# Nine of 32 experts multiply unsplit float32 weights; ranks mixed piece by piece; results collected by column halves

## The chip, the cores and the metric

One core of a Trainium2 chip runs the whole program in one launch. The metric is the device time of an execution in microseconds (us). PE is the matrix engine, PEld its weight loads, DVE, ACT and POOL are the vector, scalar and GpSimd engines, SP issues most of the DMAs.

## The reference

Two transformer blocks follow each other. The first ends in a mixture of experts, and that is what the change touches:

```
logits = h @ w_router + b_router            # 512 tokens, 32 experts
top 4 experts of each token, gates = softmax of their logits
f[token] = sum over its 4 experts e of gate * ((swiglu(h @ w1[e] + b1[e])) @ w2[e] + b2[e])
# w1[e]: [1024, 2048], w2[e]: [1024, 1024], all float32
x = layer_norm(alpha * x + gt2 * f)
```

`swiglu` clamps pairs of columns, multiplies a sigmoid with them and leaves 1024 columns. All 32 experts' weights are read: 32 x 12 MB.

## The kernel before

**Ranks and rows.** The experts are sorted by how many tokens chose them. `CAP` (line 1246) gives the rank its rows: 192 for ranks 0 to 5, 128 for ranks 6 to 14, 64 for ranks 15 to 31. A rank of 192 is worked as a block of 128 and a block of 64.

**Tiles and pieces.** `Weights` (line 1282) streams weights as tiles `wraw` of two chunks of 128 rows by 512 columns (512 KB). Seven such buffers exist. `split` (line 1299) makes two float32r parts of each tile: ACT rounds it into `whi` (L1308), DVE (736 of the 1024 columns, L1312) and POOL (288, L1313) subtract into `wlo`. Up to three tiles are split ahead of their use. Four tiles are a piece: an expert has four pieces of the first product (0 to 3) and two of the second (4, 5), 24 tiles in all, so the stage has 768 tiles.

**Products.** `mm_part` (line 1669) makes, for each of a tile's two chunks, products of 128x512 in float32r: rows' high part by `whi` (L1675), by `wlo` (L1676), and, for a block of 128 rows, rows' low part by `whi` (L1678). For a block of 64 rows both parts lie side by side in one stationary operand, and two products do. So a tile takes 4 products for a rank of 64, 6 for 128, 10 for 192. A piece of the first product begins with a small product that adds the bias (L1803). `swiglu` (line 1680) follows, and its result is transposed and split (L1666, L1667); `down` (line 1811) scales the second product by the gate and splits it into `y`.

**Order.** `sequence` (line 1254) puts ranks into groups and `order` (line 1269) writes down by hand the order of a group's pieces; A, B, C are the ranks of the group. Before: six groups of [192, 64, 64] rows, and between them two of [128, 128] and five of [128, 64]:

```
[192, 64, 64]   A0 B0 B1 A1 B2 B3 A2 C0 C1 A3 B4 C2 C3 A4 B5 A5 C4 C5
[128, 64]       A0 A1 B0 A2 B1 A3 B2 B3 A4 A5 B4 B5
```

A rank's token rows are fetched by an indirect DMA from POOL into `xg` (L1649, three buffers) and transposed on PE (L1662); a table `at`, made in `experts` (line 1755), says before which piece. After a group's last piece, `collect` (line 1864) adds its results to the tokens' accumulators: products with one-hots (L1879) and additions on DVE (L1888).

Of the kernel before, what the change touches and what calls it, by code (L numbers as in the profile page):

```python
# [22 lines left out]
def consts1():  # L23
# [6 lines left out]
    dft = np.concatenate([np.cos(ph)[:, :257] * s, np.sin(ph)[:, 1:256] * s], 1).astype(np.float32)      # [512, 512]  # L30
    dfc = np.concatenate([np.cos(pc), np.sin(pc)], 1).astype(np.float32)          # [64, 128]
# [6 lines left out]
    m = np.concatenate([strict, incl, -strict], 1)                                        # [64 s, (a | r | -a) t]  # L38
    m = np.concatenate([m, m], 0)                                                # both halves of the rows
# [11 lines left out]
def rsqrt(nc, x, y, h, t):  # L51
    """x [p, m] -> 1/sqrt(x) in place, by three steps of Newton's."""
# [33 lines left out]
def ahead(loads, parts):  # L86
    """Each load one part ahead of its use."""
# [11 lines left out]
class Blk1:  # L99
# [13 lines left out]
    # ---- parameters  # L113
    def params(self, tmp):
# [26 lines left out]
        # derived columns  # L141
        self.mq = c.tile([128, 32], F, name="muq")          # mu / 4, 1 - mu
# [15 lines left out]
    # ---- modulation  # L158
# [100 lines left out]
    def memory(self, pool):  # L259
        """Pieces: the second block's memory, its rows normed and transposed -> memD."""  # L260
# [37 lines left out]
    def stats(self, x, pool):  # L298
        """mean and 1/std columns of the rows of x [128, 1024]"""
# [7 lines left out]
    def front(self):  # L307
        tc, nc, I, c = self.tc, self.nc, self.i, self.c
        self.x0 = self.dram.tile([512, 1024], F, name="x0D")
        with tc.tile_pool(name="fh", bufs=1) as hp, tc.tile_pool(name="ft", bufs=1) as tmp, tc.tile_pool(name="fw", bufs=2) as wp:  # L310
# [4 lines left out]
            with tc.tile_pool(name="fx", bufs=1) as xp, tc.tile_pool(name="fwa", bufs=4) as wr:  # L315
# [10 lines left out]
                # alpha (gains, biases) on all partitions  # L326
# [48 lines left out]
            def shift(pl, pcx, ch, dst_l, dst_c):  # L375
                """Token shift of the channels ch of the projections (psums), to the destinations."""
# [26 lines left out]
            def group(c0, n, ctx, evac):  # L403
                """Parts for the channels c0 .. c0+n; evac(j, psum lat, psum ctx)"""
# [54 lines left out]
            def spill(dst, j, t):  # L459
                """Channels t [128, ctx | lat] -> parts of 128 tokens in the order of either direction."""  # L460
# [53 lines left out]
    def norm_keys(self, pool, spill):  # L514
        """kn = k k_k / max(|k k_k|, 1e-12) per head"""
# [31 lines left out]
    def get(self, u, k):  # L547
        return self.U[u][k] if u < 6 else []
# [31 lines left out]
    def ttile(self, shape, name):  # L580
        """Tiles of 4 KB, in turn; some of their places come with the second pool."""
# [12 lines left out]
    def unit(self, u):  # L594
        """The parts of two chunks of either direction (n = direction, chunk) that don't need the state."""
# [10 lines left out]
        def lora(i):  # L606
            def f():
                w, src, nm = ((self.w2[0], self.lw, "sw"), (self.w2[1], self.la, "a"))[i]
                dst = S[nm] = self.tt(nm)
                for d in range(2):  # L610
# [9 lines left out]
                    for hp in range(4):  # L620
                        # sigmoid(x) = (1 + tanh(x / 2)) / 2; the halves of the biases are in hb
# [88 lines left out]
        def solve(a, b):  # L710
            # even rows on the first half of the partitions, odd rows on the second
# [67 lines left out]
    def chain(self, S):  # L779
        """The steps over the chunks, in pieces."""  # L780
# [120 lines left out]
    def fourier(self):  # L901
        """Pieces of the Fourier mixing."""
# [26 lines left out]
        def third(ch, s):  # L929
            # cosines for the first half of the places (they are even), sines (odd)  # L930
# [19 lines left out]
    def rsqrt(self, x, n, eps, pool):  # L950
        """x [128, m] sums over n -> 1/sqrt(mean + eps), in place."""
# [6 lines left out]
    def gn_consts(self, p, rk):  # L958
        """Gains and bonus weights by rows, the gates' weights, in p [128, 2048] and rk [128, 2, 4, 8]."""
# [82 lines left out]
    def gn_pieces(self):  # L1042
        """Pieces of the group norm for all units but the last."""
# [71 lines left out]
    def output(self, rw, gn, W, pool, h2, hT, setup, each):  # L1115
        """x1 = LN(alpha x0 + gt1 mixed) -> DRAM, h2 = x1 (1 + sc2) + sh2 -> h2 and transposed hT; each(t) follows.
        rw: room for the parts of the recurrent half of the mixed channels; gn: what is left of it and the Fourier half."""
# [27 lines left out]
        def mm(p, t, kk, w, first, last):  # L1145
            """Two chunks from kk on."""
# [16 lines left out]
        # (W gives the weights in this order) the Fourier half of either columns, the recurrent half  # L1163
# [80 lines left out]
# rows that a rank gets without a branch: 128 + 64, 128, 64  # L1244
# [8 lines left out]

def sequence():
    """Ranks in groups worked on together, so that products and loads keep step; the first rank is known before the routing."""
    h, m, l = ([r for r in range(32) if CAP[r] == c] for c in (192, 128, 64))
    three = [[r, l.pop(0), l.pop(0)] for r in h]
    two = [[r, l.pop(0)] if l else [r] for r in m]
    one = [g[0] for g in two if len(g) == 1]
    two = [one[i:i + 2] for i in range(0, len(one), 2)] + [g for g in two if len(g) == 2]  # L1260
# [7 lines left out]
def order(g):  # L1268
    """Pieces of a group's products: 0 for the first, 1 for the second, rank, columns."""
    if len(g) == 1:  # L1270
        text = "A0 A1 A2 A3 A4 A5"
    elif len(g) == 2:
        text = "A0 A1 B0 A2 B1 A3 B2 B3 A4 A5 B4 B5"
    elif g[0] == 0:
        text = "A0 A1 B0 B1 B2 A2 B3 C0 A3 C1 B4 C2 C3 A4 B5 A5 C4 C5"
    else:
        text = "A0 B0 B1 A1 B2 B3 A2 C0 C1 A3 B4 C2 C3 A4 B5 A5 C4 C5"
# [1805 lines left out]
```

## Time and profile before

| | |
|---|---|
| runs | 3830.72, 3824.44, 3829.01 us, median 3829.01 us |
| profiled execution, span from first to last instruction | 3830.3 us |
| its own time against the median | the span is 1.3 us above the median and 0.4 us below the slowest run |
| busy over the span | PE 3391.2 (89%), DVE 2819.2 (74%), POOL 2035.1 (53%), ACT 1888.8 (49%) |
| experts' stage, first to last expert product | 822.1 to 2422 us |

The page cuts the span into 40 slices of 96 us; the experts' stage is slices 9 to 25. A line of the view by stretches holds the stretch and its length, then for PE, PEld, DVE, ACT and POOL the busy time and the number of instructions, then PE's granted clock as a share of 2.4 GHz, the busy share of the DMA engines and GB/s. A line by group holds line, engine, operation, out<-in, shapes, the count, the busy time, the mean ns of one, and the idle time ahead of them with what ended it. PE's instructions overlap, so what one costs in a row of them is the distance between starts.

### The profile page before, as it was taken

How to read it: one execution, taken by the hardware profiler on the slowest of the kernel's cores; microseconds unless marked ns; L12 is line 12 of the kernel's file. 1: busy time of each engine (PE TensorE's matmuls, PEld its weight loads, DVE VectorE, ACT ScalarE, POOL GpSimd, SP SyncE). 2: the span in 40 equal slices, each digit the busy share in tenths (PEclk: the TensorE clock that was granted, in tenths of full speed). 3: DMA queues.
4: the chain of work that ended last, by engine and by line, in shares of the span. 5: the costliest groups of instructions: out<-in, count | busy, mean ns of one | idle time of the engine just before them, and what ended most of it. 6: DMA issues, size and time to landing. Idle time of an engine off the chain costs nothing. (4 is left out here: it accounts for less than half of the span.)

```text
span 3830.3 us, 53524 instructions
## 1 busy us (share of the span) xinstructions
PE 3391.2 (89%) x17300; PEld 2590.0 (68%) x17300; DVE 2819.2 (74%) x5095; ACT 1888.8 (49%) x3153; POOL 2035.1 (53%) x1734
## 2 busy tenths in 40 slices
PE   7967689858998998888989887699999999999999
PEld 4756567645666766665666664488878878877887
DVE  6778865668998989998998988855566445555653
ACT  4634323235666666666666665443444434443442
POOL 4444323447678877887877887623242332334223
PEclk9976767868999999999999998899999999999999
DMA  7853243636788878888888887522231134223112
GB/s 253 263 138 82 65 102 91 210 118 224 250 266 262 289 258 274 274 266 262 269 283 258 261 270 259 178 82 81 72 86 50 56 122 121 78 67 90 44 50 105
DMA packets 420662, 654.00 MB, mean 171 GB/s; under 512 B 83939, under 2 KB 145568, under 8 KB 419862
## 3 DMA queue, kind: packets, MB, share of 16 engines
q1 hardware_dynamic: 414650, 633.32, 52.6%
q0 software_dynamic: 4000, 13.90, 1.2%
q8 instruction: 139, 2.28, 0.2%
q10 hardware_dynamic: 1724, 3.28, 0.2%
q14 instruction: 149, 1.22, 0.1%
HBM read 610.80 MB, written 39.61 MB: 170 GB/s over the span
## 5 line engine op out<-in xcount | busy, mean ns | idle before, releaser
L1313 POOL TENSOR_TENSOR wlo<-wraw,whi 128x288 fp32r<-128x288 f32 x952 | 1181.1, 1256 | 843.4 <-ACT whi L1308 777.6
L1312 DVE TENSOR_TENSOR wlo<-wraw,whi 128x736 fp32r<-128x736 f32 x952 | 1082.3, 1150 | 260.0 <-ACT whi L1308 255.1
L1308 ACT ACTIVATE whi<-wraw 128x1024 fp32r<-128x1024 f32 x952 | 978.7, 1053 | 398.3 <-PE psg L2251 122.5
L1676 PE MATMUL ps<-wlo,x 128*128 128x512 f32 x1216 | 525.9, 432 | 79.2 <-DVE wlo L1312 54.4
L1675 PE MATMUL ps<-whi,x 128*128 128x512 f32 x1216 | 516.8, 427 | 1.3 <-ACT whi L1308 1.1
L2249 PE MATMUL psg<-whi,xh 128*128 128x512 f32 (+1 forms) x1152 | 472.6, 410 | 1.5 <-ACT xh L2266 1.5
L2251 PE MATMUL psg<-whi,xl 128*128 128x512 f32 (+1 forms) x1152 | 451.7, 392 | 0.0
L2250 PE MATMUL psg<-wlo,xh 128*128 128x512 f32 (+1 forms) x1152 | 450.2, 391 | 0.0
L1676 PEld LDWEIGHTS ps<-wlo,x 128*128 128x128 f32 x1216 | 242.4, 199 | 200.1 <-DVE wlo L1312 108.6
L1675 PEld LDWEIGHTS ps<-whi,x 128*128 128x128 f32 x1216 | 243.0, 200 | 83.4 <-issue 20.0
L1676 PE MATMUL ps<-wlo,a 128*128 128x512 f32 x608 | 255.9, 421 | 42.3 <-DVE wlo L1312 22.9
L1698 POOL TENSOR_TENSOR ln<-ln,sg 64x256 f32<-64x256 f32 (+1 forms) x152 | 232.0, 1526 | 91.3 <-DVE ln L1697 65.9
L1675 PE MATMUL ps<-whi,a 128*128 128x512 f32 x608 | 249.5, 411 | 0.6 <-ACT whi L1308 0.6
L2251 PEld LDWEIGHTS psg<-whi,xl 128*128 128x128 f32 x1152 | 217.9, 189 | 42.4
L2249 PEld LDWEIGHTS psg<-whi,xh 128*128 128x128 f32 x1152 | 218.3, 189 | 36.4 <-ACT xh L2266 2.5
L2250 PEld LDWEIGHTS psg<-wlo,xh 128*128 128x128 f32 x1152 | 218.3, 189 | 34.6
L1678 PE MATMUL ps<-whi,x 128*128 128x512 f32 x480 | 192.7, 402 | 0.0
L1676 PEld LDWEIGHTS ps<-wlo,a 128*128 128x128 f32 x608 | 116.7, 192 | 102.4 <-DVE wlo L1312 44.5
L2389 ACT ACTIVATE pexp<-pss,mx 128x128 f32<-128x128 f32 x192 | 101.0, 527 | 154.6 <-DVE mx L2384 66.6
L1696 ACT ACTIVATE sg<-gl 64x256 f32<-64x256 f32 (+1 forms) x152 | 63.0, 415 | 169.9 <-DVE gl L1694 169.5
L1675 PEld LDWEIGHTS ps<-whi,a 128*128 128x128 f32 x608 | 116.8, 192 | 27.1 <-ACT whi L1308 2.3
L1879 PE MATMUL ps<-y,ot 128*128 128x512 f32 x424 | 117.7, 400 | 1.3 <-DVE y L1837 1.3
(732 smaller groups left out, 6828.3 us busy)
## 6 DMA issues: line engine op xcount, KB each, us to landing
wraw<-in_w SPq DMA_DIRECT2D x768, 512.0 KB
wraw<-in_w_in SPq DMA_DIRECT2D x140, 512.0 KB
mraw<-in_w_ada SPq DMA_DIRECT2D x32, 512.0 KB
wraw<-in_w_out SPq DMA_DIRECT2D x24, 512.0 KB
wada<-in_w_ada SPq DMA_DIRECT2D x16, 512.0 KB
wraw<-in_w_mem_kv SPq DMA_DIRECT2D x16, 512.0 KB
wraw<-in_w_branch_m SPq DMA_DIRECT2D x8, 512.0 KB
wraw<-in_w_branch_b SPq DMA_DIRECT2D x8, 512.0 KB
```

The lines of the kernel that those rows point to most:

```text
L1308: nc.scalar.activation(hi, raw, AF.Copy)
L1312: nc.vector.tensor_tensor(lw[:, :m], rw[:, :m], hw[:, :m].bitcast(F), op=OP.subtract)
L1313: nc.gpsimd.tensor_tensor(lw[:, m:], rw[:, m:], hw[:, m:].bitcast(F), op=OP.subtract)
L1675: nc.tensor.matmul(ps, a, hi[:, k], start=s, stop=False)
L1676: nc.tensor.matmul(ps, a, lo[:, k], start=False, stop=e and len(x) == 1)
L1678: nc.tensor.matmul(ps, x[1][:, k0 + k], hi[:, k], start=False, stop=e)
L1698: nc.gpsimd.tensor_tensor(ln[:m], ln[:m], sg[:m], op=OP.mult)
L1879: nc.tensor.matmul(p[cc], ot[j][:, t * 128:(t + 1) * 128], part[:, cc * 512:(cc + 1) * 512], start=j == 0 and i == 0, stop=j == n - 1 and ...
L2249: nc.tensor.matmul(p, xh[:, kk], hi[:, k, :n], start=kk == 0, stop=False)
L2250: nc.tensor.matmul(p, xh[:, kk], lo[:, k, :n], start=False, stop=False)
L2251: nc.tensor.matmul(p, xl[:, kk], hi[:, k, :n], start=False, stop=kk == kch - 1)
L2389: nc.scalar.activation(p[:, :n], s[:, :n], AF.Exp, bias=nm, scale=-1.0, accum_out=H["d"][:, i:i + 1])
```

## The change

- Ranks of 128 rows (9 of 32) no longer split anything ahead of the products: `whole(r)` marks them. Their weight tiles go to PE as they land, their rows and `swiglu` results stay one float32 tile, and each chunk is one float32 product instead of three float32r ones. Bias products and `y` stay as they are.
- Groups: six of [192, 64, 128, 64], two of [64, 128, 64], one of [64, 128]; nine collections instead of 13.
- `ahead` counts only tiles that are to be split against the three allowed ahead, and looks four tiles ahead at most.
- `y` is a tile per column half, and `collect` runs once per half. `xg` has two buffers instead of three.

```diff
+def whole(r):
+    return CAP[r] == 128
 def sequence():
     h, m, l = ([r for r in range(32) if CAP[r] == c] for c in (192, 128, 64))
-    three = [[r, l.pop(0), l.pop(0)] for r in h]
-    two = [[r, l.pop(0)] if l else [r] for r in m]
...
+    three = [[r, l.pop(0), m.pop(0), l.pop(0)] for r in h]
+    three[0] = [three[0][i] for i in (0, 2, 1, 3)]
+    two = []
+    while m:
+        two.append([l.pop(0), m.pop(0)] + ([l.pop(0)] if len(l) > len(m) else []))
 def order(g):
+    if len(g) == 2:
+        text = "A0 B0 A1 A2 B1 A3 B2 B3 A4 B4 A5 B5"
+    elif len(g) == 3:
+        text = "A0 B0 A1 B1 A2 A3 B2 C0 C1 B3 C2 C3 A4 B4 C4 A5 B5 C5"
     elif g[0] == 0:
+        text = "A0 A1 B0 B1 A2 B2 C0 A3 C1 B3 C2 C3 D0 D1 D2 A4 D3 B4 C4 D4 A5 B5 C5 D5"
+    else:
+        text = "A0 B0 A1 B1 A2 B2 A3 B3 C0 D0 C1 D1 C2 D2 C3 D3 A4 B4 C4 D4 A5 B5 C5 D5"
...
     def ahead(self, loads, splits):
...
-        while len(self.splits) < min(self.used + splits, len(self.parts)):
-            self.splits.append(self.split(self.loads[len(self.splits)]))
+        isplit = lambda j: self.parts[j][-1] is not False
+        n = sum(isplit(j) for j in range(self.used, len(self.splits)))
+        while len(self.splits) < min(len(self.loads), self.used + self.reach):
+            j = len(self.splits)
+            if isplit(j):
+                if n >= splits:
+                    break
+                n += 1
+            self.splits.append(self.split(self.loads[j]) if isplit(j) else self.loads[j][0])
...
-    def mm_part(self, ps, x, hi, lo, k0, first, last):
+    def mm_part(self, ps, x, w, k0, first, last, kn=None):
...
+            if not x.split:
+                nc.tensor.matmul(ps, a, w[:, k], start=s, stop=e)
+                continue
...
-        self.tbufs, self.gbufs = 5, 3
+        self.tbufs, self.abufs, self.gbufs = 5, 6, 2
...
-                get = max([first[r] - 9, 0] + [unp[q] + 1 for q in oldr])
+                get = max([first[r] - 9, 0 if r == seq[0][1] else 2] + [unp[q] + 1 for q in oldr])
...
-            if (a, r, cc) == order(g)[-1]:
+            if a == 1 and r == [q for b, q, h in order(g) if (b, h) == (1, cc)][-1]:
```

**PE, first product of a rank of 128 rows.** `x` are its rows, `ps` its result. Before (the bias, one tile, the start of the next):

```order
L1803 MATMUL ps_13063<-mb1_5881,permr_6437 128x512
L1675 MATMUL ps_13063<-whi_13031,x_12453 128x512
L1676 MATMUL ps_13063<-wlo_13032,x_12453 128x512
L1678 MATMUL ps_13063<-whi_13031,x_12454 128x512
L1675 MATMUL ps_13063<-whi_13031,x_12453 128x512
L1676 MATMUL ps_13063<-wlo_13032,x_12453 128x512
L1678 MATMUL ps_13063<-whi_13031,x_12454 128x512
L1675 MATMUL ps_13063<-whi_13044,x_12453 128x512
```

In the change (piece C0 of a group of four, then the start of D0, a rank of 64):

```order
L1833 MATMUL ps_15700<-mb1_5881,permr_6437 128x512
L1702 MATMUL ps_15700<-wraw_15580,x_15448 128x512 x2
...
L1702 MATMUL ps_15700<-wraw_15600,x_15448 128x512 x2
...
L1702 MATMUL ps_15700<-wraw_15635,x_15448 128x512 x2
L1702 MATMUL ps_15700<-wraw_15652,x_15448 128x512 x2
...
L1833 MATMUL ps_15764<-mb1_5881,mhalf1_5880 128x512
L1706 MATMUL ps_15764<-whi_15715,x_15633 128x512
L1707 MATMUL ps_15764<-wlo_15716,x_15633 128x512
```

Four tiles are now eight products straight from `wraw`, and pieces of unsplit and split tiles take turns.

**POOL, the fetch of rows (`xg`) at the end of a group.** Before, the fetches for the next group of [192, 64, 64]:

```order
L1649 DMA xg_12930<-hD_6337,idxi_6367 64x1024
L1313 TENSOR_TENSOR wlo_12525<-wraw_12432,whi_12524 128x288
L1313 TENSOR_TENSOR wlo_12549<-wraw_12457,whi_12548 128x288
L1313 TENSOR_TENSOR wlo_12560<-wraw_12481,whi_12559 128x288
L1313 TENSOR_TENSOR wlo_12571<-wraw_12505,whi_12570 128x288
L1313 TENSOR_TENSOR wlo_12582<-wraw_12522,whi_12581 128x288
L1313 TENSOR_TENSOR wlo_12603<-wraw_12546,whi_12602 128x288
L1649 DMA xg_12999<-hD_6337,idxi_6367 64x1024
```

In the change, at the same place of a group of four (`xg_13272` are the rows of the next group's B):

```order
L1329 TENSOR_TENSOR wlo_13190<-wraw_13140,whi_13189 128x288
L1674 DMA xg_13272<-hD_6337,idxi_6367 64x1024
L1329 TENSOR_TENSOR wlo_13210<-wraw_13159,whi_13209 128x288
L1674 DMA xg_13340<-hD_6337,idxi_6367 128x1024
L1329 TENSOR_TENSOR wlo_13228<-wraw_13165,whi_13227 128x288
L1674 DMA xg_13405<-hD_6337,idxi_6367 64x1024
```

The fetches now stand among the splits of the piece that PE is working on.

**PE, where it reads those rows.** In the change (L1687 are transposes; `xg_12918` lies in the buffer before, and `xg_13272` takes the buffer of `xg_12916`):

```order
L1687 MATMUL ps_13236<-ident_60,xg_12916 128x128
L1687 MATMUL ps_13249<-ident_60,xg_12918 128x64 x4
L1687 MATMUL ps_13265<-ident_60,xg_12918 128x64 x4
L1707 MATMUL ps_13206<-wlo_13190,a_12403 128x512
L1706 MATMUL ps_13206<-whi_13189,a_12403 128x512
L1707 MATMUL ps_13206<-wlo_13190,a_12403 128x512
L1706 MATMUL ps_13206<-whi_13209,a_12403 128x512
L1707 MATMUL ps_13206<-wlo_13210,a_12403 128x512
L1706 MATMUL ps_13206<-whi_13209,a_12403 128x512
L1707 MATMUL ps_13206<-wlo_13210,a_12403 128x512
L1706 MATMUL ps_13206<-whi_13227,a_12403 128x512
L1702 MATMUL ps_13277<-wraw_13176,a_12444 128x512
L1707 MATMUL ps_13206<-wlo_13228,a_12403 128x512
L1706 MATMUL ps_13206<-whi_13227,a_12403 128x512
L1707 MATMUL ps_13206<-wlo_13228,a_12403 128x512
L1702 MATMUL ps_13277<-wraw_13176,a_12444 128x512
L1687 MATMUL ps_13282<-ident_60,xg_13272 128x64 x4
```

Between the last read of the buffer's old rows and the first of its new ones there are 8 transposes, 11 products of split tiles and 2 of an unsplit one. The same stands at the start of five groups.

## Rows read from the trace of the kernel before

**Rows 1.** By stretches: six groups of ranks, and the whole experts' stage
```profile
822.10:997.00 174.90, 145.46 (x618) 102.31 (x618) 145.92 (x246) 98.67 (x134) 119.33 (x97) 0.85 0.66 209
...
1247.10:1339.10 92.00, 89.04 (x381) 65.72 (x380) 89.68 (x109) 61.32 (x79) 76.19 (x62) 1.00 0.88 287
...
1578.30:1726.10 147.80, 134.11 (x537) 93.74 (x536) 141.60 (x181) 102.69 (x141) 121.02 (x97) 0.98 0.84 271
...
2214.20:2306.40 92.20, 82.33 (x318) 57.78 (x317) 82.06 (x106) 57.99 (x77) 75.36 (x57) 0.93 0.83 269
2306.40:2422.00 115.60, 90.22 (x316) 59.04 (x315) 90.45 (x109) 60.57 (x79) 89.08 (x64) 0.88 0.70 231
...
822.10:2422.00 1599.90, 1421.84 (x5710) 990.83 (x5711) 1445.93 (x1943) 1013.47 (x1355) 1241.40 (x988) 0.95 0.80 259
```

**Rows 2.** Waits of SP's queue from 815 to 2430 us: total, times, longest
```profile
SPq L1296 <- DVE wlo L1312: 794.7, 662, 15.6
```

**Rows 3.** Groups by shape, 815 to 2430 us: the splits
```profile
L1313 POOL TENSOR_TENSOR wlo<-wraw,whi 128x288 fp32r<-128x288 f32 x765 | 936.6, 1243 | 246.7 <-ACT whi L1308 215.2 <-PE ps L1675 10.9 <-PE ps L1676 6.2
L1312 DVE TENSOR_TENSOR wlo<-wraw,whi 128x736 fp32r<-128x736 f32 x764 | 875.5, 1162 | 59.7 <-ACT whi L1308 55.7 <-PE ps L1676 1.5
L1308 ACT ACTIVATE whi<-wraw 128x1024 fp32r<-128x1024 f32 x767 | 783.1, 1051 | 151.2 <-PE ps L1675 62.5 <-issue 24.1 <-POOL wlo L1313 20.7
```

**Rows 4.** The same view: DVE's other work for blocks of 64 and 128 rows
```profile
L1697 DVE SCALAR_TENSOR_TENSOR ln<-ln,gl 64x256 f32<-64x256 f32 x92 | 64.2, 698 | 0.8
L1888 DVE TENSOR_TENSOR acc<-acc,ps 128x512 f32<-128x512 f32 x96 | 62.3, 674 | 2.8 <-PE ps L1879 2.7
L1688 DVE TENSOR_TENSOR us<-us,ps 64x512 f32<-64x512 f32 x92 | 61.8, 672 | 20.4 <-ACT us L1687 20.4
L1694 DVE TENSOR_SCALAR gl<-us 64x256 f32<-64x256 f32 x92 | 61.1, 665 | 0.5
L1837 DVE TENSOR_TENSOR y<-us,y 64x512 fp32r<-64x512 f32 x46 | 46.2, 1004 | 1.5
L1697 DVE SCALAR_TENSOR_TENSOR ln<-ln,gl 128x256 f32<-128x256 f32 x60 | 44.7, 744 | 0.5
L1695 DVE TENSOR_SCALAR ln<-us 64x256 f32<-64x256 f32 x92 | 41.6, 452 | 0.0
L1833 DVE SCALAR_TENSOR_TENSOR us<-ps,gatec,us 64x512 f32<-64x512 f32 x46 | 33.9, 737 | 7.8 <-ACT us L1832 7.7
...
L1667 DVE TENSOR_TENSOR a<-ps,a 128x128 fp32r<-128x128 f32 x92 | 25.6, 278 | 17.6 <-ACT a L1666 17.5
L1694 DVE TENSOR_SCALAR gl<-ps 128x256 f32<-128x256 f32 x60 | 24.9, 414 | 8.1 <-PE ps L1678 7.8
L1695 DVE TENSOR_SCALAR ln<-ps 128x256 f32<-128x256 f32 x60 | 24.6, 409 | 0.0
L1667 DVE TENSOR_TENSOR a<-ps,a 128x256 fp32r<-128x256 f32 x60 | 24.3, 409 | 2.5 <-ACT a L1666 2.5
```

**Rows 5.** PE in order of time: start, length; float32r products in a row
```profile
1346.27 0.40 PE L1675 MATMUL ps<-whi,x 128*128 128x512 f32 x1
1346.50 0.40 PE L1676 MATMUL ps<-wlo,x 128*128 128x512 f32 x1
```

**Rows 6.** By line, ns min/median/max, first and last start: float32 products, full and half clock
```profile
L1027 PE MATMUL ps<-gnc,gdl x4: 590/592/594, 702.7 to 704.0; 128*128 128x512 f32 x4
...
L910 PE MATMUL ps<-xl x4: 1057/1057/1057, 581.0 to 583.6; 64*64 64x512 f32 x4
```

**Rows 7.** By stretches of 20 us: where the DMA engines are full
```profile
1240.00:1260.00 20.00, 18.31 (x78) 12.93 (x77) 19.68 (x23) 16.63 (x21) 16.15 (x13) 1.00 1.01 323
```

**Rows 8.** The tile xg, 815 to 2430 us: its indirect DMAs
```profile
DMA to landing us min/median/max: 5.0/7.5/10.0
```

**Rows 9.** By stretches: the stage before the experts
```profile
400.00:800.00 400.00, 316.83 (x2442) 252.77 (x2442) 275.16 (x634) 114.20 (x230) 140.13 (x145) 0.73 0.42 121
```

More of the change, by code (lines that the diff above doesn't have):

```diff
@@ L1251 @@
 AHEAD = 2
+def whole(r):
+    return CAP[r] == 128
 def sequence():
     h, m, l = ([r for r in range(32) if CAP[r] == c] for c in (192, 128, 64))
-    three = [[r, l.pop(0), l.pop(0)] for r in h]
-    two = [[r, l.pop(0)] if l else [r] for r in m]
-    one = [g[0] for g in two if len(g) == 1]
-    two = [one[i:i + 2] for i in range(0, len(one), 2)] + [g for g in two if len(g) == 2]
+    three = [[r, l.pop(0), m.pop(0), l.pop(0)] for r in h]
[3 more added lines that the diff above has]
+        two.append([l.pop(0), m.pop(0)] + ([l.pop(0)] if len(l) > len(m) else []))
+    assert not l
     out = []
@@ L1292, in load @@
         raw = raw or self.raw.tile([128, self.kn, 512], F, name="wraw")
+        kn = raw.shape[1]
         o = 0
@@ L1650, in gather, with rows_tiles @@
         return x
-    def rows_tiles(self, name, n):
-        return [self.x.tile([128, 8, 128], R, name=name, tag=name, bufs=self.tbufs) for _ in range(2 if n == 128 else 1)]
+    def rows_tiles(self, name, n, split=True, bufs=None):
+        m = 2 if n == 128 and split else 1
+        return Rows([self.x.tile([128, 8, 128], R if split else F, name=name, tag=name, bufs=bufs or self.tbufs) for _ in range(m)], n, split)
     def transposed(self, src, n, x, k0):
@@ L1659, in transposed @@
         p = self.psum()
-        m = 128 if len(x) == 2 else 64
+        m = x.n
         for k in range(n):
@@ L1748, in parts @@
         def parts(r, a, cc):
-            return [(lambda: [ew(r)[a][:, cc * 512:(cc + 1) * 512]], k0) for k0 in range(0, 8, kn)]
+            return [(lambda: [ew(r)[a][:, cc * 512:(cc + 1) * 512]], k0, not whole(r)) for k0 in range(0, 8, kn)]
         first = [(lambda m=m: [m], k0) for m, k0 in before]
@@ L1787, in unpack @@
             for x, (_, _, m) in zip(xg[r], blocks(r)):
-                p = self.rows_tiles("x", m)
+                p = self.rows_tiles("x", m, not whole(r))
                 for k0 in (0, 4):
@@ L1795, in up @@
             half = self.halves[where[r]]
-            if cc == 0:
+            if cc == 0 and not whole(r):
                 nc.gpsimd.tensor_copy(half[:, 0:64], self.perm[:, r:r + 1].bitcast(F).to_broadcast([64, 64]))
             for k0 in range(0, 8, kn):
-                hi, lo = self.W.next()
+                w = self.W.next()
                 for p, xx in zip(ps, x):
                     if k0 == 0:
-                        pm = half if len(xx) == 1 else self.perm[:, r:r + 1].to_broadcast([64, 128])
+                        pm = half if xx.n == 64 else self.perm[:, r:r + 1].to_broadcast([64, 128])
                         nc.tensor.matmul(p, pm, self.b1[:, cc * 512:(cc + 1) * 512], start=True, stop=False)
-                    self.mm_part(p, xx, hi, lo, k0, False, k0 + kn == 8)
+                    self.mm_part(p, xx, w, k0, False, k0 + kn == 8)
                 self.flush(1)
@@ L1816, in down, with full @@
                 self.need(r)
-                ys[r] = [[x_.tile([128, 1024], R, name="y", tag="y", bufs=6) for _ in range(2 if m == 128 else 1)] for _, _, m in bl]
+            y = ys[r, cc] = [[x_.tile([128, 512], R, name="y", tag="y", bufs=12) for _ in range(2 if m == 128 else 1)] for _, _, m in bl]
             ps = [self.psum() for _ in bl]
             for k0 in range(0, 8, kn):
-                hi, lo = self.W.next()
+                w = self.W.next()
                 for p, a in zip(ps, acts[r]):
-                    self.mm_part(p, a, hi, lo, k0, k0 == 0, k0 + kn == 8)
+                    self.mm_part(p, a, w, k0, k0 == 0, k0 + kn == 8)
                 self.flush(1)
-            cs = slice(cc * 512, (cc + 1) * 512)
-            def whole(p, y, g):
-                nc.scalar.activation(y[0][:, cs], p, AF.Copy, scale=g)
-                nc.vector.scalar_tensor_tensor(y[1][:, cs], p, g, y[0][:, cs].bitcast(F), op0=OP.mult, op1=OP.subtract)
+            def full(p, y, g):
+                nc.scalar.activation(y[0], p, AF.Copy, scale=g)
+                nc.vector.scalar_tensor_tensor(y[1], p, g, y[0].bitcast(F), op0=OP.mult, op1=OP.subtract)
             def half(p, y, g):
@@ L1835, in parts @@
                 def parts():
-                    nc.scalar.activation(y[0][0:64, cs], u, AF.Copy)
-                    nc.vector.tensor_tensor(y[0][64:128, cs], u, y[0][0:64, cs].bitcast(F), op=OP.subtract)
+                    nc.scalar.activation(y[0][0:64], u, AF.Copy)
+                    nc.vector.tensor_tensor(y[0][64:128], u, y[0][0:64].bitcast(F), op=OP.subtract)
                 self.put_off(None, parts)
-            for p, y, (b, _, m) in zip(ps, ys[r], bl):
-                self.put_off(None, lambda f=whole if m == 128 else half, p=p, y=y, b=b: f(p, y, gate[:, b:b + 1]))
+            for p, yy, (b, _, m) in zip(ps, y, bl):
+                self.put_off(None, lambda f=full if m == 128 else half, p=p, y=yy, b=b: f(p, y, gate[:, b:b + 1]))
         fin = {}
@@ L1904, in experts @@
         for r in ranks:
-            m = sum(2 if b[2] == 128 else 1 for b in blocks(r))
+            m = sum(2 if b[2] == 128 and not whole(r) else 1 for b in blocks(r))
             tiles += [r] * m
@@ L1926, in experts @@
         gs = groups()
-        where = {r: min(j, 1) for g in seq for j, r in enumerate(g)}
+        where = {r: min(sum(not whole(q) for q in g[:j]), 1) for g in seq for j, r in enumerate(g)}
+        ots = {}
         def begin():
@@ L1947, in experts @@
                     self.need(r)
-                    acts[r] = [self.rows_tiles("a", m) for _, _, m in blocks(r)]
+                    acts[r] = [self.rows_tiles("a", m, not whole(r), self.abufs) for _, _, m in blocks(r)]
                 up(r, cc)
@@ L2016, in overflow @@
                     x = self.gather(hD, ix[:, 0:1])
-                    xp = [x_.tile([128, 8, 128], R, name="xo", tag="xg", bufs=self.gbufs) for _ in range(2)]
-                    ap = self.rows_tiles("a", 128)
+                    xp, ap = [self.rows_tiles("a", 128, bufs=self.abufs) for _ in range(2)]
                     for k0 in (0, 4):
```

118 lines of the change are left out of this document (57 added, 61 removed).

## The prediction

> **What bounds the kernel now.** I read the slices first, then the stretches by group of ranks, then the groups by shape. The experts' stage runs 1599.9 us, and in it DVE is busy 1445.9 us, nine tenths; the DMA engines are busy 0.80 of the time at 259 GB/s, and PE's granted clock is 0.95 [rows 1]. PE's 1421.8 us look as full, but its products overlap: each lasts 0.40 us and the next starts after 0.23 [rows 5], so 4368 expert and 424 collecting products fill 4792 x 0.23 = 1102 us. In a group of [192, 64, 64] DVE fills 141.6 of 147.8 us, a share of 0.958. SP's queue, which issues the weight loads, waits 794.7 us for DVE's half of the split to free a buffer [rows 2], so the loads are late because the split is late. The split is also DVE's largest work: 875.5 us in 764 calls of 1162 ns. POOL needs 1243 ns and ACT 1051 ns for their share of a tile [rows 3]. So the stage is bound by DVE in front of a DMA that is near its own limit.
>
> **What the change removes.** Nine ranks of 24 tiles are not split any more: 216 tiles. On DVE that is 216 x 1.162 = 251 us, on POOL 216 x 1.243 = 268 us, on ACT 216 x 1.051 = 227 us [rows 3]. The `swiglu` results of these ranks lose their subtraction, 36 x 0.409 = 15 us, and nine collections instead of 13 save 32 additions of 0.674 us, 22 us [rows 4]. DVE's total falls from 1446 to about 1158 us, and something else must set the pace.
>
> **What the unsplit product costs PE.** Four float32 products of 512 columns start from 702.7 to 704.0 us: three distances of 0.43 us [rows 6]. So a tile of a 128-row rank falls from 6 x 0.23 = 1.38 to 2 x 0.43 = 0.86 us. The same kind of product at half clock has distances of (583.6 - 581.0) / 3 = 0.87 us; the cost lies between 0.43 and 0.87 us, and I take 0.43 because the stage's clock is 0.93 to 1.00 after its first group [rows 1]. The Trainium skill speaks against the change here: "FP8 and Floating Point Precision", section "TensorE Precision Notes", has true float32 as four passes through the array. By it an unsplit product would cost four float32r ones, 0.92 us, the unsplit tile more than the split one, and the sum would be near 3704 us. The trace disagrees: at full clock its rows show less than two.
>
> **What a tile costs the DMA.** A tile is 524,288 bytes. The 20 us in which the engines are full (1.01) move 323 GB/s [rows 7], that is 1.62 us a tile; the best whole group moves 287 GB/s, 1.83 us [rows 1]. Before, the slower split hid this. I take 1.62, since the groups' own rates at shares of 0.83 to 0.88 scale to the same 323 to 326 GB/s, and keep 1.83 as the other end.
>
> **The sum, group by group.** The new order makes stretches with different limits, and the seven buffers even out only some 11 us of load, so each stretch is taken by its own slowest engine.
>
> - Group of four, pieces A and B of the first product, eight tiles a pair, all split. DVE: 8 x 1.162 = 9.3; a block of 128 rows 0.414 + 0.409 + 0.744 + 0.409 = 1.98; two blocks of 64 rows, each 0.672 + 0.665 + 0.452 + 0.698 + 0.278 = 2.77 [rows 4]; together 16.8 us. PE needs 56 x 0.23 = 12.9, the DMA 13.0. At the share of 0.958 that DVE reaches, 17.5 us; four pairs 70.2 us.
> - Pieces C and D: only D is split. DVE 4 x 1.162 + 1.57 + 2.77 = 9.0, PE 8 x 0.43 + 16 x 0.23 = 7.1, DMA 8 x 1.62 = 13.0. The DMA sets it: four pairs 51.9 us.
> - Second product, one column half, 16 tiles: PE 72 x 0.23 + 8 x 0.43 + 28 collecting products x 0.23 = 16.6 + 3.4 + 6.4 = 26.4; DMA 26.0; DVE 12 x 1.162 + 3 x (0.737 + 1.004) + 2 x 0.737 + 4 x 0.674 = 23.3. PE just sets it: two halves 52.8 us.
> - Together 174.9 us, six times 1049.4. Before, 148 us for 72 tiles; now 175 us for 96.
> - Two groups of [64, 128, 64], 72 tiles: DMA 116.9 (DVE 48 x 1.162 + 8 x 2.77 + 4 x 1.57 + 14 = 98, PE about 72): 233.7 us. The last group, 48 tiles: 77.9 us.
> - Kept from before: the first group runs 174.9 - 147.8 = 27.1 us longer than its like, while routing work still runs, and the last 115.6 - 92.2 = 23.4 us [rows 1].
> - Fetches. With two `xg` buffers the fetch of the next group's B can only be issued when PE has read the rows before, and PE transposes its result 11 split and 2 unsplit products later, 11 x 0.23 + 2 x 0.43 = 3.4 us. Issue to landing takes 7.5 us [rows 8]. PE waits about 4 us, five times, 20 us. Queued behind the fetch on POOL are the splits of the same piece. At the lower end (nothing) the transposes would run late enough; at the upper (10.0 us to land) 33 us.
>
> Sum: 1049.4 + 233.7 + 77.9 + 27.1 + 23.4 + 20 = 1431.5 us against 1599.9: 168.4 us less. From the profiled execution's 3830.3 that is 3661.9; the median of the runs lies 1.3 lower, so 3661 us. Costed at nothing: the collections by column halves (the same 424 products, spread over more pieces, under a PE that has room except in the second product), ACT (its 227 us saved lie under DVE), and everything after the stage, whose instructions are not touched.
>
> **The rivals.**
>
> *The transfers are already at their limit.* For it: no whole group moved more than 287 GB/s though SP had loads waiting. Against: SP was waiting for buffers, not for the wire [rows 2]. Price: 384 tiles x 0.20 = 78 us where the DMA sets the pace, and 16 x 1.83 - 26.4 = 2.8 us in each of 12 halves, 34: 3661 + 112 = 3773.
>
> *The buffers even everything out.* Then the longest total binds: 768 x 1.62 = 1246 us of DMA (DVE 1158), plus 27.1, 23.4 and 20: 1317, time 3546. Against: seven buffers cover 11 us, and the A and B stretch is 70 us long.
>
> *The float32 product costs 0.87 us a time.* At half clock it does, and at full clock it would if the array goes over float32 more often than the four products show. A second-product half is then 16.6 + 7.0 + 6.4 = 30.0 on PE, 3.6 x 12 = 43 us more: 3704. The C and D pairs stay under the DMA at 10.6. The Trainium skill's four passes, cited above, are this case.
>
> *The clock falls for the whole stage, and it gets slower.* Place: PE, in C and D pieces, where it waits on the DMA and its work is thinner. For it: the stage before the experts, with PE busy 317 of 400 us in short products, was granted 0.73 [rows 9]. Against: groups with PE busy at nine tenths or a little under it kept 0.93 [rows 1]. PE's products need 3496 x 0.23 + 432 x 0.43 = 990 us at full clock; with the 70 us of start, end and fetches, it decides when 990 / clock passes 1530, a mean clock under 0.65. At 0.60 the stage is 1720: 3949.
>
> *The change's own waits eat it.* An unsplit tile holds its buffer until PE has used it, no longer freed three tiles ahead by the split. If that and the fetches starved the loads in every group by 28 us, nothing would be left: no difference.
>
> **How the numbers follow.** What a measurement here can tell from no change is about 0.2%, 7.7 us. Forecast 0.68; transfers at their limit 0.13; buffers even out 0.09; dear float32 product 0.03; clock 0.05; waits eat it 0.02. All but the last two are faster: 0.93; same 0.02; slower 0.05. The range starts at 3590, half way into the evened-out case (3661 to 3546 has its middle at 3603) with a little room for cheaper splits when POOL and DVE meet less, and ends at 3775, where the slow transfers end. Outside lie most of the evened-out case and the last two, under 0.2.
>
> **What would show it.** Splits fall by 216 on each of ACT, DVE and POOL. The unsplit products start 0.43 us apart. The stage ends near 2250 us; its DVE share falls from 0.90 to about 0.8 and the DMA share rises to about 0.9. Groups of four take near 175 us: DVE full in A and B, the DMA full in C and D. PE shows waits of about 4 us for `xg` at five places. It is wrong if the stage's GB/s stay under 290 while DVE is idle (first rival), if the clock in C pieces is 0.5 (third and fourth), or if PE's longest waits are for fetches.

## The result and the profile after

| | before | after |
|---|---|---|
| median of the runs | 3829.9 us (4 runs) | 3787.0 us (3783.5 to 3795.3, 4 runs) |
| ratio | | 0.9887, 95% interval 0.987 to 0.9904 |
| span of the profiled execution | 3830.3 us | 3793.5 us |
| experts' stage | 1599.9 us | 1570.0 us |

The change gains 43 us. The prediction said 168 and 3661 us, with a range that ended at 3775. The profiled execution of after was the slowest of its four runs, 3795.3 us, 8 us above their median.

The view by stretches of the kernel after: ahead of the stage, the stage, what follows it, and then one group of four, one of [64, 128, 64] and another of four.

```profile
0.00:816.80 816.80, 619.72 (x4444) 486.98 (x4444) 597.34 (x1208) 296.56 (x582) 326.90 (x296) 0.77 0.50 149
816.80:2386.80 1570.00, 1455.39 (x5261) 911.45 (x5261) 1132.04 (x1641) 823.06 (x1140) 939.91 (x761) 0.95 0.80 265
2386.80:3793.50 1406.70, 1349.23 (x7162) 1112.10 (x7160) 780.94 (x1945) 577.26 (x1216) 467.88 (x452) 0.98 0.28 83
1050.30:1247.00 196.70, 182.48 (x689) 121.21 (x688) 143.39 (x226) 107.59 (x149) 120.72 (x99) 0.97 0.79 262
1247.00:1379.10 132.10, 121.51 (x401) 69.38 (x400) 95.95 (x131) 68.64 (x98) 80.71 (x67) 0.95 0.87 290
1379.10:1569.60 190.50, 183.51 (x674) 117.67 (x673) 148.81 (x197) 109.17 (x152) 120.38 (x101) 0.96 0.85 280
```

Against [rows 1], DVE's busy time in the stage falls from 1446 to 1132 us, a little further than the prediction worked out (1158). Its share falls from 0.90 to 0.72, not to 0.8, because the stage did not follow. The DMA share stays at 0.80, and PE's busy time rises by 34 us, though 432 float32 products stand in the place of 1296 float32r ones. No engine is full over the stage. The splits, by line, against [rows 3]; these rows hold the whole span, where before has 952 of each:

```profile
L1329 POOL TENSOR_TENSOR wlo<-wraw,whi 128x288 fp32r<-128x288 f32 x736 | 957.3, 1311 | 1001.7 <-ACT whi L1324 935.2
L1328 DVE TENSOR_TENSOR wlo<-wraw,whi 128x736 fp32r<-128x736 f32 x736 | 828.5, 1133 | 472.4 <-ACT whi L1324 458.5
L1324 ACT ACTIVATE whi<-wraw 128x1024 fp32r<-128x1024 f32 x736 | 769.9, 1056 | 609.8 <-DMA wraw<-in_w 193.3
...
L1702 PE MATMUL ps<-wraw,x 128*128 128x512 f32 x576 | 277.4, 634 | 0.0
L1702 PE MATMUL ps<-wraw,a 128*128 128x512 f32 x288 | 138.3, 619 | 0.0
```

Each engine makes 216 splits fewer. The last two rows are the unsplit products: 576 and 288, **864 records for 432 products** (216 tiles of two chunks). The timeline of PE shows one tile of two products, and then the eight products of a piece:

```profile
1121.89 1.98 PE L1702 MATMUL ps<-wraw,x 128*128 128x512 f32 x4
...
1163.36 7.13 PE L1702 MATMUL ps<-wraw,x 128*128 128x512 f32 x16
1170.33 0.65 PE L1687 MATMUL ps<-ident,ln 128*128 128x128 f32 x4
1175.84 0.51 PE L1687 MATMUL ps<-ident,ln 128*128 128x128 f32 x2 [4.86 <-POOL ln L1728]
1176.28 0.79 PE L1833 MATMUL ps<-mb,mhalf 64*128 64x512 f32 x1
1177.00 0.80 PE L1706 MATMUL ps<-whi,x 128*128 128x512 f32 x1
1177.59 0.63 PE L1707 MATMUL ps<-wlo,x 128*128 128x512 f32 x1
1178.02 0.63 PE L1706 MATMUL ps<-whi,x 128*128 128x512 f32 x1
...
1179.62 0.39 PE L1706 MATMUL ps<-whi,x 128*128 128x512 f32 x1
1179.85 0.39 PE L1707 MATMUL ps<-wlo,x 128*128 128x512 f32 x1
```

Sixteen records last 7.13 us together and one alone 0.59, so they start (7.13 - 0.59) / 15 = 0.436 us apart. A product takes two of them: 0.87 us, where the prediction took 0.43. The rows below show the second cost. After piece C3, PE stands still for 4.86 us until POOL has made `ln`, the last step of `swiglu`, and then it runs at half clock for a while: the granted clock from 1176.3 to 1179.2 us is 0.50, and the starts are 0.43 us apart where 0.23 is its pace [rows 5]. The waits of PE over the stage, before:

```profile
PE ps L1676 <- DVE wlo L1312: 77.3, 110, 5.2
...
PE ps L1662 <- POOL ln L1698: 49.1, 25, 6.5
PE ps L1676 <- POOL wlo L1313: 41.6, 38, 3.7
```

and after:

```profile
PE ps L1687 <- POOL ln L1728: 56.8, 19, 6.8
PE ps L1707 <- DVE wlo L1328: 30.4, 39, 3.5
PE ps L1687 <- DMA xg<-hD,idxi: 16.4, 6, 4.2
PE ps L1707 <- POOL wlo L1329: 7.0, 12, 1.1
```

The waits for the two parts of the split fell from 77 and 42 to 30 and 7 us, as they should. The 57 us for `ln` are the largest now, in fewer and longer waits than the 49 of before, and the prediction has no line for them.

### The profile page after: what moved, and what is told of

Same layout as the page of the kernel before. It is cut to its first block, busy times and chain, and to the rows that moved or that the text cites. A ratio compares the mean times of both kernels' runs of the same rounds, so it can differ in the third digit from the quotient of the medians.

```text
span 3793.5 us, 51274 instructions
## 1 busy us (share of the span) xinstructions
PE 3424.3 (90%) x16864; PEld 2510.5 (66%) x16864; DVE 2510.3 (66%) x4793; ACT 1696.9 (45%) x2937; POOL 1734.7 (46%) x1509
## 5 line engine op out<-in xcount | busy, mean ns | idle before, releaser
L1329 POOL TENSOR_TENSOR wlo<-wraw,whi 128x288 fp32r<-128x288 f32 x736 | 957.3, 1311 | 1001.7 <-ACT whi L1324 935.2
L1328 DVE TENSOR_TENSOR wlo<-wraw,whi 128x736 fp32r<-128x736 f32 x736 | 828.5, 1133 | 472.4 <-ACT whi L1324 458.5
L1324 ACT ACTIVATE whi<-wraw 128x1024 fp32r<-128x1024 f32 x736 | 769.9, 1056 | 609.8 <-DMA wraw<-in_w 193.3
L1707 PE MATMUL ps<-wlo,x 128*128 128x512 f32 x928 | 383.7, 413 | 29.9 <-DVE wlo L1328 25.6
L1706 PE MATMUL ps<-whi,x 128*128 128x512 f32 x928 | 393.6, 424 | 1.0 <-ACT whi L1324 0.8
L1702 PE MATMUL ps<-wraw,x 128*128 128x512 f32 x576 | 277.4, 634 | 0.0
L1728 POOL TENSOR_TENSOR ln<-ln,sg 64x256 f32<-64x256 f32 (+1 forms) x152 | 166.5, 1096 | 163.9 <-DVE ln L1727 107.7
L1706 PEld LDWEIGHTS ps<-whi,x 128*128 128x128 f32 x928 | 179.5, 193 | 72.1 <-issue 23.3
L1702 PEld LDWEIGHTS ps<-wraw,x 128*128 128x128 f32 x576 | 111.9, 201 | 136.2 <-issue 135.3
L1702 PE MATMUL ps<-wraw,a 128*128 128x512 f32 x288 | 138.3, 619 | 0.0
L1707 PEld LDWEIGHTS ps<-wlo,a 128*128 128x128 f32 x464 | 90.6, 195 | 47.8 <-DVE wlo L1328 16.4
```

The lines of the kernel that those rows point to most:

```text
L1324: nc.scalar.activation(hi, raw, AF.Copy)
L1328: nc.vector.tensor_tensor(lw[:, :m], rw[:, :m], hw[:, :m].bitcast(F), op=OP.subtract)
L1329: nc.gpsimd.tensor_tensor(lw[:, m:], rw[:, m:], hw[:, m:].bitcast(F), op=OP.subtract)
L1702: nc.tensor.matmul(ps, a, w[:, k], start=s, stop=e)
L1706: nc.tensor.matmul(ps, a, hi[:, k], start=s, stop=False)
L1707: nc.tensor.matmul(ps, a, lo[:, k], start=False, stop=e and not two)
```

## The experiments

All runs were made beside the kernel before; the ratios are to it. They were made in five sets, in which the median of before came out between 3829.9 and 3833.7 us, so a difference of some 5 us between runs of two sets says nothing. The theory at first was the price of the product.

**1. A cheap product.** In the change, the operands are read as bfloat16 by their upper halves, which leaves out the lower halves; one record per product then, 0.23 us.

```diff
-                nc.tensor.matmul(ps, a, w[:, k], start=s, stop=e)
+                nc.tensor.matmul(ps, a.bitcast(BF)[:, 1::2], w[:, k].bitcast(BF)[:, 1::2], start=s, stop=e)
```

> The change with one edit: each unsplit product reads the upper 16 bits of its float32 operands as bfloat16, so one pass of 128x512 takes the place of the float32 product. It leaves out the lower 16 bits of rows and weights. Counts of instructions, buffers, transfers and order stay. Theory (price): the unsplit product takes 0.86 us on PE, two records of 0.43, and not 0.43; that is what ate the gain. PE's own need in the stage then falls by 432 x (0.86 - 0.23) = 272 us, below that of the DMA; the groups fall back to DVE in A and B, the DMA in C and D and in the second product, and the time is 3640 to 3700 us. Rival (loads): the stage waits for weight tiles that sit in their buffers until PE is through with them, whatever a product costs; then little changes, 3750 to 3790.

3775.9 us, ratio 0.9859 (0.9842 to 0.9875): only 11 us less than the change, so the price alone did not eat the gain. By stretches, the first group of [64, 128, 64] and the group of four behind it:

```profile
1236.60:1387.00 150.40, 111.70 (x348) 64.25 (x353) 98.44 (x131) 67.42 (x97) 78.26 (x66) 0.77 0.81 262
1387.00:1570.20 183.20, 159.45 (x622) 107.40 (x624) 146.16 (x197) 107.96 (x152) 127.67 (x101) 0.93 0.87 287
```

The group of four falls from 190.5 to 183.2, and the one of three rises from 132.1 to 150.4: PE is granted 0.77 there, and over the stage it now waits for `ln` 149 us in 63 times. This reads as if the pieces of 128 rows were now over too soon to cover the chain of `swiglu`. The time lies in the rival's range, but its reason isn't seen: PE waits 7 us for weight tiles over the stage, and 149 for `swiglu`.

**2 and 3. The old groups.** Sequence and piece orders of before in the changed kernel; once with unsplit ranks, once with all of them split:

```diff
 def whole(r):
-    return CAP[r] == 128
+    return False
...
```

> The change with the groups and the piece orders of before ([192,64,64], [128,128], [128,64]); the nine ranks stay unsplit. Price theory: a [128,128] group needs 96 x 0.86 = 83 us of PE for its products and some 13 for the rest, so it gains nothing against 90 to 100; a [128,64] group needs 63 + 10 on PE and 78 to 88 on the DMA, and falls from 99 to about 88, five times; [192,64,64] stays. Sum 3770 to 3800: the regrouping by itself is worth little. Rival (mixing is what pays): without pieces of split and unsplit ranks in turn the DVE stands still in one group and is full in the next, nothing is gained, 3820 or more.

> The change with the old groups and every rank split: what is left of the change is the collection by column halves, two xg buffers in place of three and the new look-ahead. Costed at nothing in the prediction but for the fetches (20 us). Theory: 3822 to 3838, no difference from before. Rival: the second collection per group and the fetches cost 20 us or more, 3850 and over, which would be a second part of the missing gain.

Unsplit 3825.0 us, 0.9986 (0.9974 to 0.9998), hardly faster than before, as the rival had it. All split 3879.7 us, 1.0128 (1.0108 to 1.0147): **46 us slower than before**, with nothing left of the change but what the prediction costed at nothing or at 20 us. So the unsplit ranks are worth 55 us in the old groups, the new groups another 38, and something beside them takes 46. In the run with all split, PE's waits show it (from 817 to 2387 us, most of its stage):

```profile
PE ps L1684 <- POOL ln L1725: 54.9, 18, 6.2
...
PE ps L1684 <- DMA xg<-hD,idxi: 29.9, 6, 8.1
```

(L1684 is this kernel's L1687.) Before, PE waited for `xg` once, 2.8 us.

**4. Where unsplit ranks pay.** Ranks 12 to 14 split again, so that only groups of four hold unsplit ranks.

```diff
-    return CAP[r] == 128
+    return CAP[r] == 128 and r < 12
```

> The change with ranks 12 to 14 (in the groups [64,128,64] and [64,128]) split again; six ranks stay unsplit. PE's own need falls by 72 x 0.34 = 24 us, DVE's grows by 72 x 1.16 = 84 us in these three groups. Price theory: these groups are held by the DMA at 290 GB/s (132 us for 72 tiles), DVE at 126 of work and a share of 0.96 would need 131, so within 10 us of the change, 3780 to 3797. Rival (DVE still decides everywhere): 20 us or more slower than the change. Rival (every unsplit rank loses): faster than the change by 15 us or more.

3823.9 us, 0.9978 (0.9966 to 0.999), 37 us slower than the change, as the first rival had it:

```profile
1255.40:1403.60 148.20, 119.98 (x449) 82.58 (x448) 132.58 (x157) 91.89 (x122) 106.40 (x91) 0.90 0.81 263
1799.00:1943.50 144.50, 118.05 (x449) 80.83 (x448) 130.03 (x158) 92.04 (x122) 104.61 (x91) 0.91 0.83 266
```

DVE is busy nine tenths here, and a group takes 10 to 16 us more than unsplit. Taking work off DVE does pay, even at 0.87 us a product.

The new theory: **two `xg` buffers.** Ahead of a fetch the program calls `need` for the rank that had the buffer. `need` works off everything that is open for that rank, its rows' transposes but also its `swiglu` steps, and what stands ahead of them in the queue. With two buffers this rank is the one whose last first-product piece has just ended: rank 7's `swiglu` of C3 is forced through before D3, for the rows of rank 27, and that of rank 18 before A4. The timelines of ACT, DVE and POOL of the change show the chain that PE waits for at 1171 us; the split in its middle (L1328) is in DVE's queue ahead of the chain's next step:

```profile
1172.38 0.41 DVE L1724 TENSOR_SCALAR gl<-ps 128x256 f32<-128x256 f32 x1
1172.72 0.41 DVE L1725 TENSOR_SCALAR ln<-ps 128x256 f32<-128x256 f32 x1
1172.94 0.41 ACT L1726 ACTIVATE sg<-gl 128x256 f32<-128x256 f32 x1
1173.05 0.91 DVE L1328 TENSOR_TENSOR wlo<-wraw,whi 128x736 fp32r<-128x736 f32 x1
1173.88 1.01 DVE L1727 SCALAR_TENSOR_TENSOR ln<-ln,gl 128x256 f32<-128x256 f32 x1
1175.06 0.72 POOL L1728 TENSOR_TENSOR ln<-ln,sg 128x256 f32<-128x256 f32 x1 [0.45 <-DVE ln L1727]
```

**5 and 6. Three buffers; or rows only.** Run 5 gives the change three `xg` buffers and takes the room from `y`. Run 6 keeps two, and gives the rows' transposes a tag of their own, so that a fetch forces only them:

```diff
-        self.tbufs, self.abufs, self.gbufs = 5, 6, 2
+        self.tbufs, self.abufs, self.gbufs = 5, 6, 3
...
```

```diff
-                    self.todo.append((self.now, r, lambda x=x, p=p, k0=k0: ...
+                    self.todo.append((self.now, (r,), lambda x=x, p=p, k0=k0: ...
...
-                at[...].insert(0, lambda r=r, q=oldr: (self.need(q[-1]) if q else None, fetch(r)))
+                at[...].insert(0, lambda r=r, q=oldr: (self.need((q[-1],)) if q else None, fetch(r)))
...
```

> The change with three xg buffers, as before; the room comes from y, ten column halves in place of twelve. Theory (fetches): with two buffers a fetch can only be issued once the rank that had the buffer is transposed, and the program first finishes everything open of that rank, its swiglu results too (need ahead of the fetch); so PE stands still for xg (16 us in 6 waits) and for POOL's last step of swiglu (57 us in 19), and starts again at half clock. With three buffers the old rank is long done: 3735 to 3765. Rival (PE itself): PE needs about 1290 us of the stage and what it no longer waits here it waits elsewhere, 3775 to 3795. With fewer y buffers it could also be slower by a few us.

> The change with two xg buffers, but ahead of a fetch only the transposes of the fetched rows of the old rank are finished, not its open swiglu steps. Theory (fetches, by the flush): the waits of PE for POOL's swiglu product fall from 57 to some 20 us and the half-clock stretches behind them go too: 3745 to 3770, while the 16 us for xg stay. Rival (the steps are late anyway, since ACT, DVE and POOL have splits queued ahead of them): 3780 to 3795.

Three buffers: 3757.1 us, 0.9807 (0.9777 to 0.9838), 30 us less than the change. Rows only: 3745.6 us, 0.9774 (0.9745 to 0.9803), **41 us less**, with the waits for `ln` gone and those for `xg` left:

```profile
PE ps L1687 <- DMA xg<-hD,idxi: 15.4, 6, 4.7
...
PE ps L1687 <- POOL ln L1728: 5.3, 4, 3.5
```

**7. Buffers or halves.** The old groups, all split, with three `xg` buffers and five `a` as before.

> The old groups with every rank split and the collection by column halves, but with three xg buffers (and five of the swiglu results, as before). The same with two took 46 us more than before. If the xg buffers are the cause: 3825 to 3845. If the second collection per group is: 3865 to 3885.

3822.8 us, 0.9981 (0.9969 to 0.9993): 57 us less than with two. The second collection per group costs nothing, as the prediction had it.

**8. The loads alone.** For ranks 27 to 31 only the first tile of a piece is split and multiplied; the other three are loaded and left. The cut for the first product:

```diff
...
-                    self.mm_part(p, xx, w, k0, False, k0 + kn == 8)
+                    if r < 27 or k0 == 0:
+                        self.mm_part(p, xx, w, k0, False, k0 + kn == 8 or r > 26)
...
```

> The change, but for ranks 27 to 31 (the 64-row ranks of the groups [64,128,64] and [64,128]) only the first tile of each piece is split and multiplied; the other three are loaded and left. It leaves out that part of these ranks' products. PE then needs about 50 us of a [64,128,64] group and DVE less, so the loads alone set its time: 117 us for 72 tiles if a tile takes the DMA 1.62 us, as the prediction took, 132 us (as in the change) if it takes 1.83, as its rival had it. The run: 3745 to 3760 in the first case, 3780 to 3795 in the second.

3743.1 us, 0.9772 (0.9745 to 0.9798), 2 us below the first case. The two groups of [64, 128, 64]:

```profile
1249.60:1373.30 123.70, 97.77 (x265) 49.87 (x265) 52.52 (x97) 38.06 (x67) 27.17 (x32) 0.79 0.91 312
1768.00:1891.00 123.00, 99.86 (x265) 50.53 (x265) 51.75 (x97) 38.13 (x67) 27.97 (x32) 0.79 0.92 313
```

123 us for 72 tiles, 1.71 a tile: between 1.62 and 1.83, nearer to what the prediction took. That is a bound and not the price of a tile: the DMA engines were busy 0.91 to 0.92 of it, SP's queue waited 40 us of the first group for PE to free a buffer, and two stretches of 20 us in that group with the engines full moved 351 and 362 GB/s, 1.49 and 1.45 us a tile.

**9. Both edits together, and 10. the better kernel.** Run 9 joins 1 and 6; run 10 joins 5 and 6 with the float32 product.

> Both edits together: ahead of a fetch only rows are finished, and the unsplit product reads the upper 16 bits of its operands as bfloat16 (the lower 16 bits are left out). Theory (price and flush add up): with rows alone the change took 3746; PE's own need now falls by another 272 us under the other engines, the groups of four come near the forecast 175 and the time to 3680 to 3715. Rival (the long product is also the cover of swiglu: four tiles of 0.46 us are over before its chain of ACT, DVE, ACT, DVE and POOL is through): PE waits for POOL's product as in the first run (149 us), the clock falls in the groups of three, and the time stays at 3720 to 3760.

> Rows only ahead of a fetch, and three xg buffers with ten y halves: the candidate that beats both kernels. If the flush and the wait for xg are separate costs: 3725 to 3742, below either alone (3746 and 3757). If three buffers only took the flush away: 3740 to 3760.

Run 9: 3737.3 us, 0.9759 (0.9717 to 0.9802), 8 us less than run 6, with intervals that overlap; its rival is what came, with 107 us of waits for `ln` in 56 times. Run 10: **3725.8 us, 0.9721 (0.9682 to 0.976)**, 61 us less than the change and faster than both kernels, below either edit alone. By stretches, the same three groups as shown of after:

```profile
1035.10:1221.50 186.40, 181.41 (x690) 118.68 (x689) 144.52 (x224) 106.52 (x148) 120.20 (x99) 0.99 0.84 277
1221.50:1351.20 129.70, 119.34 (x401) 66.92 (x400) 92.21 (x132) 68.91 (x99) 81.86 (x66) 0.99 0.91 304
1351.20:1534.00 182.80, 180.31 (x673) 116.88 (x672) 144.72 (x196) 109.52 (x152) 120.99 (x101) 0.98 0.87 290
```

PE is now busy 0.92 to 0.99 of each group, at a clock of 0.98 to 0.99.

**11. The same edit in the kernel before.**

> The kernel before with one edit: ahead of a fetch only rows are finished. Its fetches come so early, with three buffers, that the old rank is done: theory 3822 to 3836, no difference, so the flush is a cost that the change brought. Rival (before paid for it too, PE waits 49 us for the same product there): 3790 to 3815.

3830.9 us, 1.0005 (0.9987 to 1.0022): no difference. The cost came with the change. The theory's reason does not quite hold, though: in the profiled executions PE's waits for `ln` did fall, from 49.1 to 26.1 us, while those for POOL's half of the split rose from 41.6 to 58.0. So there a wait for `swiglu` taken away came back in part as one for the splits.

**12. The forecast's premises together.** Run 10 with the cheap product, and `swiglu` results transposed eight tiles after the steps of `swiglu` are given out, instead of four.

> The forecast's own premises put in place together: rows only ahead of a fetch, three xg buffers (ten y halves), the unsplit product reading the upper 16 bits of its operands (the lower 16 are left out), and the swiglu results transposed eight tiles after their product's end in place of four, so that short tiles cover the chain of swiglu. Theory (the forecast left out the flush, the fetch and the product's price, and nothing else of size): groups of four 175 to 180, groups of three 120 to 127 (the loads alone took 123), the time 3660 to 3695. Rival (something else holds the stage, such as the split's own chain from landing to PE): 3705 to 3740.

3721.5 us, 0.9714 (0.9686 to 0.9742): the rival. The groups apart say more than the sum:

```profile
1031.80:1214.70 182.90, 161.83 (x642) 109.72 (x641) 144.55 (x226) 104.85 (x148) 124.31 (x99) 0.92 0.85 282
1214.70:1356.30 141.60, 109.04 (x353) 61.02 (x353) 95.72 (x132) 68.46 (x98) 81.84 (x67) 0.82 0.86 286
1356.30:1532.90 176.60, 158.12 (x626) 107.92 (x624) 138.92 (x194) 106.80 (x151) 126.36 (x100) 0.91 0.88 289
```

Groups of four reach 176 to 188 us, with the forecast's 175 for three of the five within 2 us; those of three stay at 142. Why they do is not settled. In the first of them PE waits 16 us for `ln`, 16 for the splits, and is granted 0.82; that the low clock draws the rest out was not tried alone.

## Why the prediction was wrong, point by point

The stage by groups, from the first product of a group to that of the next:

| us | forecast | after | run 10 | run 12 |
|---|---|---|---|---|
| first group of four | 202.0 | 233.5 | 216.8 | 215.1 |
| five groups of four | 874.5 | 982.5 | 926.8 | 900.2 |
| two of [64, 128, 64] | 233.7 | 266.6 | 261.2 | 284.4 |
| last, [64, 128] | 101.3 | 87.3 | 89.2 | 95.7 |
| fetches, apart | 20 | in the groups | in the groups | in the groups |
| stage | 1431.5 | 1569.9 | 1494.2 | 1495.4 |

**Bound and removal: right.** DVE bound the stage; 216 splits went from each engine; DVE's total is 1132 us for the 1158 forecast; giving 72 tiles back to it cost 37 us between medians (run 4).

**The failed step: "Fetches ... PE waits about 4 us, five times, 20 us."** The transfers were sized well: 16.4 us in six waits, and a third buffer on top of run 6 gave 20 (run 10). What the step put at nothing is the call that stands ahead of the fetch. It drains the old rank's `swiglu` as well, with PE idle for a chain of five steps over three engines and at half clock after it. With this draining alone taken out, the kernel takes 41 us less (run 6), a third of the 126 us that the forecast missed. Both edits to the fetches together gave 61 us back (run 10); in the old groups a third buffer gave 57 (run 7). In the first group, 17 of the 31 us that it was too long went with them, too. The call, `need(q[-1])`, stands in the listing of the kernel: the prediction asked what the fetch waits for, not what the waiting call does on its way.

**The unsplit product's price: wrong by a factor of two.** "Four float32 products of 512 columns" in [rows 6] were four records of two products. The rival with 0.87 us had the price right. So had the Trainium skill, "FP8 and Floating Point Precision", section "TensorE Precision Notes", which counts four passes for true float32; the trace agrees, with 0.87 us against 0.23, or 3.8 times. The prediction said that the trace disagreed, and it was the reading that did. On PE the unsplit tile is dearer than the split one, 1.74 against 1.38 us, not cheaper. The rival's place for it was right, too: the second product of a group of four, as the next table shows. In the whole time it weighs less than the rival's 43 us, since making the product cheap lengthens the other groups: from run 10 to run 12 the six groups of four get 28 us shorter, but the groups of three and of two 30 us longer. Net, the cheap product gained 11, 8 and 4 us (run 1 against after, 9 against 6, 12 against 10, where the transposes came later as well); the intervals of each pair overlap.

**Pieces of a group of four.** The mean of the five later groups, by the starts of C0 and A4 in the timelines:

| us | forecast | after | run 10 | run 12 |
|---|---|---|---|---|
| A and B | 70.2 | 71.3 | 71.4 | 70.9 |
| C and D | 51.9 | 63.4 | 54.1 | 54.2 |
| second product | 52.8 | 61.8 | 59.9 | 54.9 |

A and B were right. One group of the five takes 79 us for them in each of these runs; why stays open. C and D were too long by the fetches and the draining, and fell near the forecast without them (run 10). PE's part of a pair is 12.2 us at the least (the shortest C piece 7.7, the shortest D 4.5) where the prediction had 7.1: the dear product makes it 10.6, and bias products and transposes, which the sum left out, are the rest. That is still under the 13.0 of the DMA. The second product is 60 by the sum with the dear product, and run 10 took that; the cheap product makes it 3 to 6 us shorter in each of the five groups in all three pairs of runs. So of the 108 us that the five groups took too long, 56 went with the two edits to the fetches, and some 35 are the product's price by that sum (25 by runs 10 and 12).

**What a tile costs the DMA: not shown to be off.** The rival at 1.83 read a limit from a stretch that DVE held. The 1.62 was no limit either: the kernel before itself had moved more in another 20 us, 1.53 us a tile, and run 8 more still.

```profile
1340.00:1360.00 20.00, 20.00 (x82) 14.98 (x82) 15.40 (x20) 13.60 (x16) 16.58 (x14) 1.00 1.01 343
```

The groups of [64, 128, 64] took 132 to 135 us for the forecast's 117, and 123 in run 8; what holds them there stays open.

**Costed at nothing:** the collections by halves (run 7) and what follows the stage (1408 to 1407 us) were right.

**The other rivals.** The clock stayed at 0.95 over the stage, and the four C pieces of the group at 1050 ran at 1.00. It fell in groups of [64, 128, 64] of other runs: to 0.77 and 0.82 with the cheap product (runs 1 and 12), to 0.79 with products left out (run 8), to 0.90 with every tile split (run 4). The buffers did not even everything out: the stage took 1570 us, not 1317. The sign that was set for slow transfers, GB/s under 290 with DVE idle, did appear (265 at a share of 0.72), though in run 10 the same tiles went through in 76 us less; a rate shows what was asked of the DMA as well as what it can do. "The change's own waits eat it" named unsplit tiles that hold buffers, priced at everything or nothing, with a chance of 0.02; the mechanism that did eat much was its neighbour, the fetch.

What is left between run 10 and the forecast, 65 us, lies in the groups of four (10 us each, 7 of them in the second product, by the product's price), the first group (15) and those of three (14 each); the last group is 12 shorter than forecast, and 20 were forecast for fetches. The first group and those of three were not taken apart.

## What to carry to other kernels

A record in a profile is not an instruction: count the records of a line against the program's own instructions before a price is read from them. When a buffer is taken away, look at the code that runs ahead of the reuse and list everything that it finishes, not only what frees the buffer. And a long operation may be the cover of a latency: making it short can be worth little while the chain beside it has no other.

## What the runs showed of the hardware that was not expected

- A float32 product of 128x512 leaves two records whose starts are 0.43 us apart, with two weight loads; as bfloat16 it leaves one, 0.23 apart from the next. Both read the same 512 columns.
- A stall costs twice: after PE had stood still for 4.86 us its products started 0.43 us apart for 2.6 us more, and after one of 5.44 us for 5 us (granted clock 0.50 in both stretches, 1.00 behind them). With the stalls gone (run 10) the groups' granted clock rose from 0.95 to 0.97 up to 0.98 and 0.99.
- In the same group of three PE was granted 0.99 in run 10, busy 119 of 130 us, and 0.82 in run 12, busy 109 of 142. The product's type differs between them as well, so what the clock followed is not shown.
- A stretch with the DMA engines full is not one rate: such stretches of 20 us moved 323 and 343 GB/s in the kernel before, and 351 and 362 in run 8.
